# Gates of a hybrid block as 2x2 blocks with seven products in a stage of their own, tokens scaled first, attention and linear attention filled with other projections

## The chip, the core and the metric

The kernel runs on one core of a Trainium2 chip. The metric is the device time of one execution in microseconds (us), the median over runs. The core has five engines that run at the same time, each its own list of instructions in order: TensorE (PE: matmuls and transposes; PEld is its weight load), VectorE (DVE), ScalarE (ACT), GpSimd (POOL) and SyncE (SP, which here only issues DMA transfers). An instruction waits until the tiles it reads are written and the buffer it writes is free.

## The reference, cut to what matters

Sixteen meta tokens and 1024 frames (1040 tokens of width 1024) go through one layer: half a feed-forward block, a mix of attention and gated linear attention, half a feed-forward block.

```python
h = h + 0.5 * swiglu(rmsnorm(h, ffn1_norm), ...)                 # D_FF = 2816
u = rmsnorm(h, mix_norm)                                         # h / rms(h) * gain
(aq, ak, av, gq, gk, gv, gr, g_low, gate_a, gate_b) = split(u @ w_in)
ya = window_sink_attention(aq, ak, av, att_sinks)                # 16 chunks of 64 frames, 8 heads
log_a = log_sigmoid(g_low @ gla_gate_w + gla_gate_b) / 16
og = gated_linear_attention(gq, gk, gv, log_a)                   # 4 heads, running sums of log_a
yb = rmsnorm(og, gla_out_norm) * silu(gr)
mixed = sigmoid(gate_a) * (ya @ w_branch_att) + sigmoid(gate_b) * (yb @ w_branch_gla)
h = h + mixed @ w_out
h = h + 0.5 * swiglu(rmsnorm(h, ffn2_norm), ...)
return rmsnorm(h, final_norm)[:, 16:]
```

`gate_a` and `gate_b` are 1024 columns wide each, the widest parts of `w_in`; `gq` and `gk` have 256, `gv`, `gr` and `aq` 512, `ak` and `av` 128, `g_low` 16.

## The kernel before

Features lie on the 128 partitions, tokens along the rows. A float32 operand is split into a high and a low part, and each product takes three matmuls: high weight by high token, high weight by low token, low weight by high token. In the source this is `mm` (L97, L98, L99; tiles `pj` for a projection, `br` for a branch), with 8 input tiles: a *unit* of one projection tile (128 columns) over 512 tokens is 24 matmuls of 128x512. Tokens come in chunks of 512, 512 and 16 or 512, 256 and 272.

Both feed-forward blocks (FFN1 to about 728 us, FFN2 from about 1350 us) work by 2x2 blocks of weights and tokens with seven products instead of eight (`Seven`, `Group`; L515, tiles `pb`, `pa`, `pd`). The sums of weight blocks come from VectorE or GpSimd, and each sum is split by a ScalarE cast (L291) and a VectorE subtraction (L292).

The mix between them runs so:

1. In the last products of FFN1 (L840) `add_half` (L403) updates `h`, and `Norm.put` (L131) writes gain times `h` as `u2h` and `u2l`. The sums of squares (L862) give the RMS factor only after the first projections (`total`, `spread`), and every projection is multiplied by it on VectorE when it leaves PSUM.
2. K, V, Q of the attention; then 16 attention chunks (`turn`, `scores`, `values`, `attend`), each with one gate-A unit (`fill.pop(0)()`) between its parts. The gate goes to DRAM (`gates`).
3. Attention branch, then `g_low`, `gk`, `gq`, `gv`. `heads[0].decays()` (matmuls `z` L1279, then a chain over ScalarE, VectorE and GpSimd that ends in `kd`, the tile `d` of L1298, in `gq` of L1302 and `gk` of L1304) is issued before the last projections.
4. Linear attention: two pairs of heads, each `begin` (transposes `km`, `kt`), `products(0)`, `state`, and 8 steps. A step has one gate-B unit, then `products(j + 1)` (`at`), then `step(j)` (`go`, `kv`). `heads[1].decays()` is issued after the first `state`.
5. Output gate (`gr`), branch of linear attention, `w_out`, FFN2.

A scheduler orders instructions when the program is built. PSUM has 8 banks, handed out in turn by `bank(...)`. `ttile` takes one of 4 temporary buffers.

Of the kernel before, what the change touches and what calls it, by code (L numbers as in the profile page):

```python
# [35 lines left out]
def hybrid_kernel(  # L36
# [67 lines left out]


    def tiles_of(c0, n):
        return [(t, P if t < S // P else NM) for t in range(c0 // P, (c0 + n + P - 1) // P)]

    class Norm:

        def __init__(self, g, name, pool=None, cols=T):
            self.g, self.name, self.pool, self.cols = g, name, pool, cols
            self.hi = [None] * KT
            self.lo = [None] * KT
            self.acc = None
            self.tot = sml.tile([P, 9], F32, tag="tot", name=f"{name}t", bufs=2)

        def open(self, m):  # L120
            self.hi[m] = atile(f"{self.name}h{m}", F32R, self.pool, self.cols)
            self.lo[m] = atile(f"{self.name}l{m}", F32R, self.pool, self.cols)
            if m == 0:
                self.acc = atile(f"{self.name}q", F32, self.pool, self.cols)

        def put(self, m, c0, n, h):

            g = vec[:, self.g + m:self.g + m + 1]
            hi, lo = self.hi[m][:, c0:c0 + n], self.lo[m][:, c0:c0 + n]
            nc.scalar.activation(hi, h, AF.Copy, scale=g)  # L130
            nc.vector.scalar_tensor_tensor(lo, h, g, hi.bitcast(F32), op0=ALU.mult, op1=ALU.subtract)  # L131

        def total(self, c0, n):

            ps = bank("tot")
            for t, w in tiles_of(c0, n):
                nc.tensor.matmul(ps[0:w, t:t + 1], self.acc[:, t * P:t * P + w], ones[:, 0:1], start=True, stop=True)
            self.root(c0, n, ps)

        def root(self, c0, n, tot):  # L140

            ts = tiles_of(c0, n)
            for lo, hi, w in ((ts[0][0], min(ts[-1][0] + 1, 8), P), (8, ts[-1][0] + 1, NM)):
                if lo < hi:
                    r = self.tot[0:w, lo:hi]
                    nc.scalar.activation(r, tot[0:w, lo:hi], AF.Sqrt, bias=eps_t[0:w, :], scale=1.0 / D)
                    nc.vector.reciprocal(r, r)

        def widen(self, c0, n, dg):

            ts = tiles_of(c0, n)
            for w in (P, NM):
                mine = [t for t, v in ts if v == w]
                if mine:
                    a, k = mine[0] * P - c0, len(mine)
                    nc.vector.tensor_copy(
                        dg[0:w, a:a + k * P].rearrange("p (a b) -> p a b", b=P),
                        self.tot[0:w, mine[0]:mine[0] + k].unsqueeze(2).to_broadcast([w, k, P]))

        def spread(self, c0, n, dg=None):  # L160

            ps = bank("rep")
            if dg is None:
                dg = ttile("dg")
                self.widen(c0, n, dg)
# [1465 lines left out]
```

## Time and profile before

| what | value |
|---|---|
| median of 3 runs | 2053.46 us (2052.05 to 2054.71) |
| the profiled execution | 2056.41 us, of which the span of the trace is 2054.7 us |
| granted TensorE clock, mean over the span | 0.992 |
| busy share of the span | PE 99%, DVE 66%, ACT 41%, POOL 10% |
| instructions | PE 12177, DVE 2305, ACT 1599, POOL 222 |

The span goes from the first to the last instruction; the rest of an execution's time lies around it. A busy share is an average over stages whose limits differ. A granted clock of 1.00 is 2.4 GHz, 0.50 is 1.2 GHz.

### The profile page before, as it was taken

What the parts mean: (1) busy time and instruction counts of PE and PEld (TensorE: products, weight loads), DVE (VectorE), ACT (ScalarE), POOL (GpSimd) and SP (SyncE); (2) the same over time, 40 slices, a digit from 0 to 9 for tenths busy, and PEclk for the clock granted to TensorE, in tenths of its full rate; (3) what the DMA queues carried; (4) which work ended last, traced back from release to release, by engine and by line L of the source; (5) the groups of instructions that cost most, each with busy time, mean ns of one, the idle gap of its engine ahead of it and who ended that gap; (6) DMA issues with size and microseconds to landing.
All of it is one profiled execution on the core that took longest, in us unless ns stands there. A gap on an engine that the chain in (4) does not pass through costs nothing.

```text
span 2054.7 us, 31806 instructions
## 1 busy us (share of the span) xinstructions
PE 2024.0 (99%) x12177; PEld 1801.9 (88%) x12177; DVE 1359.7 (66%) x2305; ACT 835.0 (41%) x1599; POOL 195.2 (10%) x222
## 2 busy tenths in 40 slices
PE   8899999999999999999999999999999999999998
PEld 7899999999999998888897778888888888878888
DVE  5866677666688775774435336568876776757885
ACT  5534444444322354664224323244544544442223
POOL 1000000001223060000100000120000000022212
PEclk9999999999999999999999999999999999999999
DMA  6333344349976231126211225641543443699722
GB/s 206 106 112 128 125 161 161 125 146 343 351 280 221 80 88 54 58 60 187 76 52 57 62 67 175 219 139 44 185 161 123 168 160 125 206 374 347 279 92 83
DMA packets 271690, 317.74 MB, mean 155 GB/s; under 512 B 23975, under 2 KB 187937, under 8 KB 271537
## 3 DMA queue, kind: packets, MB, share of 16 engines
q1 hardware_dynamic: 253888, 254.30, 37.6%
q10 hardware_dynamic: 17296, 61.29, 7.9%
q8 instruction: 96, 1.57, 0.3%
q0 software_dynamic: 352, 0.11, 0.1%
q14 instruction: 58, 0.47, 0.1%
HBM read 208.01 MB, written 107.63 MB: 154 GB/s over the span
## 4 chain that ended last, share of the span: by engine, by line
PE 92%; DMA 4%; DVE 2%; ACT 1%; issue 1%; SPq 0%; DVEq 0%; POOLq 0%; ACTq 0%
PE pb L515 30%; PE pd L515 15%; PE pa L515 7%; PE pj L97 6%; PE pj L98 6%; PE pj L99 6%; PE br L97 1%; PE br L99 1%; PE br L98 1%; PE wo L97 1%; PE wo L98 1%; PE wo L99 1%; PE pd L840 1%; DMA tm<-f2mid 1%; PE tp L1096 1%; DMA f1mid<-kl 1%
## 5 line engine op out<-in xcount | busy, mean ns | idle before, releaser
L515 PE MATMUL pb<-tt,wop 128*128 128x260 f32 (+1 forms) x2016 | 337.8, 321 | 0.0
L515 PEld LDWEIGHTS pb<-tt,wop 128*128 128x128 f32 x2016 | 294.9, 188 | 28.1
L515 PE MATMUL pb<-tm,wop 128*128 128x260 f32 (+1 forms) x1440 | 238.4, 322 | 7.0 <-DVE h L403 3.6
L291 ACT CAST wop<-s 128x512 fp32r<-128x512 f32 x232 | 144.0, 622 | 227.3 <-PE pb L515 97.9
L515 PEld LDWEIGHTS pb<-tm,wop 128*128 128x128 f32 x1440 | 210.4, 191 | 27.1 <-ACT h L458 4.1
L97 PE MATMUL pj<-u2h,whi 128*128 128x512 f32 (+2 forms) x608 | 229.4, 377 | 2.9 <-DVE o L1350 1.7
L98 PE MATMUL pj<-u2l,whi 128*128 128x512 f32 (+2 forms) x608 | 224.5, 369 | 0.0
L99 PE MATMUL pj<-u2h,wlo 128*128 128x512 f32 (+2 forms) x608 | 224.4, 369 | 0.0
L292 DVE TENSOR_TENSOR wop<-s,wop 128x512 fp32r<-128x512 f32 x232 | 166.2, 718 | 87.0 <-ACT wop L291 86.4
L291 ACT CAST wop<-raw 128x512 fp32r<-128x512 f32 x174 | 108.3, 623 | 219.6 <-PE pb L515 104.9
L499 POOL TENSOR_TENSOR s<-raw 128x512 f32<-128x512 f32 x28 | 37.0, 1323 | 1059.9 <-DMA tm<-f1mid 455.2
L97 PEld LDWEIGHTS pj<-u2h,whi 128*128 128x128 f32 x608 | 114.6, 188 | 22.2 <-issue 2.2
L292 DVE TENSOR_TENSOR wop<-raw,wop 128x512 fp32r<-128x512 f32 x174 | 122.2, 704 | 12.8 <-ACT wop L291 12.4
L99 PEld LDWEIGHTS pj<-u2h,wlo 128*128 128x128 f32 x608 | 114.5, 188 | 17.1
L98 PEld LDWEIGHTS pj<-u2l,whi 128*128 128x128 f32 x608 | 114.6, 189 | 15.3
L403 DVE SCALAR_TENSOR_TENSOR h<-pb,h 128x520 f32<-128x520 f32 (+1 forms) x136 | 93.8, 693 | 41.6 <-PE pb L515 39.4
L515 PE MATMUL pd<-tm,wop 128*128 128x260 f32 (+1 forms) x720 | 118.8, 319 | 0.0
L192 ACT CAST whi<-raw 128x1024 fp32r<-128x1024 f32 x58 | 60.8, 1048 | 134.5 <-PE pj L98 76.7
L515 PE MATMUL pb<-tb,wop 128*128 128x260 f32 (+1 forms) x672 | 112.6, 321 | 0.5 <-ACT vec L88 0.5
L515 PEld LDWEIGHTS pd<-tm,wop 128*128 128x128 f32 x720 | 104.4, 189 | 9.5
L515 PE MATMUL pa<-tb,wop 128*128 128x260 f32 (+1 forms) x672 | 112.3, 320 | 0.0
L515 PE MATMUL pd<-tb,wop 128*128 128x260 f32 (+1 forms) x672 | 112.2, 320 | 0.0
(381 smaller groups left out, 3803.6 us busy)
## 6 DMA issues: line engine op xcount, KB each, us to landing
tm<-f1mid ACTq DMA_DIRECT2D x56, 520.0 KB, 6.3
tm<-f2mid ACTq DMA_DIRECT2D x56, 512.0 KB, 5.9
raw<-in_ffn_w_gate SPq DMA_DIRECT2D x42, 512.0 KB, 3.9
raw<-in_ffn_w_up SPq DMA_DIRECT2D x42, 512.0 KB, 3.9
raw<-in_ffn_w_down SPq DMA_DIRECT2D x80, 256.0 KB, 5.2
f1mid<-kh SPq DMA_DIRECT2D x70, 260.0 KB, 2.8
f1mid<-kl SPq DMA_DIRECT2D x70, 260.0 KB, 2.9
f2mid<-kh SPq DMA_DIRECT2D x70, 256.0 KB, 2.9
```

Of the source, the lines that this page charges most:

```text
L97: nc.tensor.matmul(ps, wh[k], xh[k], start=(k == 0), stop=False)
L98: nc.tensor.matmul(ps, wh[k], xl[k], start=False, stop=False)
L99: nc.tensor.matmul(ps, wl[k], xh[k], start=False, stop=(k == n - 1))
L192: nc.scalar.copy(hi[:, 0:cols], raw[:, 0:cols])
L291: nc.scalar.copy(x[:, 0:n], src)
L292: nc.vector.tensor_sub(x[:, n:2 * n], src, x[:, 0:n].bitcast(F32))
L403: nc.vector.scalar_tensor_tensor(hm, ps, 0.5, hm, op0=ALU.mult, op1=ALU.add)
L499: (eng.tensor_add if add else eng.tensor_sub)(a[s], a[x], a[y])
L515: nc.tensor.matmul(ps, y, x[:, c0 + s0:c0 + s0 + sn], start=(first and k == 0 and at == 0), stop=(at == 2 and k == len(cols) - 1), skip_gr ...
L840: nc.tensor.matmul(ps, y, x[:, c0 + s0:c0 + s0 + sn], start=(n == 0), stop=(n == 3 * LAST - 1), skip_group_check=True)
L1096: nc.tensor.transpose(ps[0:k, ga * P:(ga + 1) * P], s.p[:, ga, off:off + k], ident)
```

## The change

- **Tokens scaled first.** The last FFN1 products run half by half (512 + 8 tokens each). The squares are summed on the way, the RMS factor of a half is made (`scales_of_half`, `scales_to_rows`), and `scaled(m, c)` multiplies `h` by gain and factor in place, then splits it (`uh`, `ul`). Evictions of projections no longer multiply.
- **A stage for gates.** GK0, GK1, GV0 run with interleaved tiles (`together`). Sixteen differences of token blocks replace the blocks in place, twelve are split; then GV1, then eight `gate_pair`s make all 16 gate tiles by 2x2 blocks: 7 products of 12 matmuls of 128x512 for each pair, with sums and splits of the weights, two block sums and four sigmoids. Two token tiles are overwritten, and reloaded from DRAM afterwards.
- **Other fills.** Attention's 16 chunks now hold GV2, GV3, GQ, GR and `g_low`; the linear attention holds the attention branch in units of 12 matmuls of 128x512 (5 before, one in each of the first 8 steps, 1 in the first step of the second pair, 2 at the end) and, in four steps of the second pair, the output gate of the first pair (4 transposes each). GK, GQ, GV and GR lie in DRAM in between.

```diff
+    def scaled(m, c):
+        u = ub[m][c]
+        nc.vector.scalar_tensor_tensor(u, u, vec[:, GM + m:GM + m + 1], accs[c], op0=ALU.mult, op1=ALU.mult)
+        for to, at, n in ((c * 512, 0, 512), (S + 8 * c, 512, NM // 2)):
+            hi, lo = u_hi[m][:, to:to + n], u_lo[m][:, to:to + n]
+            nc.scalar.copy(hi, u[:, at:at + n])
+            nc.vector.tensor_sub(lo, u[:, at:at + n], hi.bitcast(F32))
...
+    for c in range(2):
+        for m in range(KT):
...
+                if m == 2:
+                    dgs[0] = scales_of_half(0, double("tot"))
+                if m == 4:
+                    ps = double("rep")
+                    scales_to_rows(0, (ps, ps[:, 512:]), dgs[0])
+                if m > 4:
+                    scaled(m - 5, 0)
...
+    hooks = {k: (lambda k=k: scaled(k, 0)) for k in range(3, KT)}
+    hooks[2] = second_scales
+    together([0, 1], CH_T[0:1], hooks)
+    scales_to_rows(1, (bank("rep"), bank("rep")), dgs[1])
+    for m in range(KT):
+        scaled(m, 1)
+    together([2], CH_T[0:1])
+    together([0, 1, 2], CH_T[1:])
...
+        nc.vector.tensor_sub(b11[k], b12[k], b11[k])
+        nc.vector.tensor_sub(b12[k], b22[k], b12[k])
+        nc.vector.tensor_sub(b22[k], b22[k], b11[k])
+        nc.vector.tensor_sub(b21[k], b21[k], b22[k])
+    for n, bs, first in (("T2", b22, True), ("T1", b11, True), ("T3", b12, False)):
+        for k in range(4):
+            g8.tops[n][k] = g8.halves(g8.operand(first, "tt"), bs[k])
+    hw[3] = ktiles(wt.cut(wt.raw(plain_views[3])))
+    for ch in CH_T:
+        together([3], [ch])
...
+    def gate_pair(m):
...
+        b = product(0)
+        x11, x22 = g8.block("x11"), g8.block("x22")
+        nc.scalar.copy(x11, b)
+        a = product(1)
+        nc.vector.tensor_add(x11, a, x11)
+        g.sums(nc.vector)
+        keep(0, 0, x11, x11)
+        product(2)
...
+    for m in range(0, 16, 2):
...
+        gate_pair(m)
...
-    for m in range(KT):
-        fill += project_units(cols_view(w_in, C_GA + m * P), CH_FR, spill_gate(m, False))
+    for i in (2, 3):
+        us = project_units(cols_view(w_in, C_GV + i * P), CH_T, ev_tok(i))
+        slots += [us[0:1], us[1:3]]
...
+    for p in range(2):
+        for x, src, n in (("k", gk_dram[p], T), ("q", gq_dram[p], S), ("v", gv_dram[2 * p], S), ("w", gv_dram[2 * p + 1], S)):
+            ins[x, p] = atile(f"g{x}{p}")
+            nc.sync.dma_start(out=ins[x, p][:, 0:n], in_=src)
...
-    heads = [Gla(0)]
-    heads[0].decays()
-    heads.append(Gla(1))
-    heads[0].values()
-    heads[1].values()
...
+    heads = [Gla(0), Gla(1)]
+    heads[0].decays()
+    for _ in range(5):
+        fill.pop(0)()
+    for p in range(2):
+        g = heads[p]
+        g.begin()
+        g.products(0)
+        g.state()
+        if p == 0:
+            heads[1].decays()
+        for j in range(8):
+            if j % 2 == 0 or p == 0:
+                if len(fill) > 2:
+                    fill.pop(0)()
+            if p == 1 and j in (1, 3, 5, 7):
+                out_gate(j // 4, CH_FR[(j // 2) % 2:(j // 2) % 2 + 1])
+            if j < 7:
+                g.products(j + 1)
+            g.step(j)
```

Over the whole program TensorE has 96 matmuls of 128x512 fewer (768 of gate units go, 672 of gate pairs come).

On VectorE, the list of the changed kernel before the first matmul of GV1 reads so; `tt` is the split of a difference of token blocks (`h2`), `g` the copy of transposed GV0 tokens, and `wlo_9159` the low weight of GV1.

```order
L229 TENSOR_TENSOR tt_9132<-h2_5957,tt_9132 128x512
L229 TENSOR_TENSOR tt_9135<-h2_5959,tt_9135 128x512
L229 TENSOR_TENSOR tt_9138<-h2_6230,tt_9138 128x512
L229 TENSOR_TENSOR tt_9141<-h2_6232,tt_9141 128x512
L889 COPY g_9069<-vt_9068 128x512
L229 TENSOR_TENSOR tt_9144<-h2_6033,tt_9144 128x512
L229 TENSOR_TENSOR tt_9147<-h2_6035,tt_9147 128x512
L229 TENSOR_TENSOR tt_9150<-h2_6310,tt_9150 128x512
L229 TENSOR_TENSOR tt_9153<-h2_6312,tt_9153 128x512
L126 TENSOR_TENSOR wlo_9159<-raw_9156,whi_9158 128x1024
```

In the kernel before, a projection's low weight had no token work of this kind ahead of it; here all sixteen differences and twelve splits stand ahead of `wlo_9159`.

On TensorE, the linear attention of the kernel before begins so: `km`, `kt` are transposes of `kd` (`d`), and the last `pj` rows of GV stand ahead of them; `z` is the second pair's.

```order
L98 MATMUL pj<-u2l_8653,whi 128x272
L99 MATMUL pj<-u2h_8652,wlo 128x272
L1227 MATMUL vt<-ident,v 128x128 x3
L1311 MATMUL km<-ident,d 16x128
L1317 MATMUL kt<-ident,d 128x128 x8
L1335 MATMUL at<-gq_11346,gk_11345 128x128 x2
L1327 MATMUL kv<-gvm_11244,km 64x128
L1327 MATMUL kv<-gvm_11245,km 64x128
L1279 MATMUL z<-glow,gw 128x384 x2
L1279 MATMUL z<-glow,gw 128x272
```

And in the changed kernel (`br` is a unit of the attention branch; the first pair's `z` stands 60 matmuls `br` ahead of `km`, right behind the last matmul of the attention):

```order
L97 MATMUL br<-qs_10412,whi 128x512
L98 MATMUL br<-qs_10411,wlo 128x512
L1398 MATMUL km<-ident,d 16x128
L1404 MATMUL kt<-ident,d 128x128 x8
L1422 MATMUL at<-gq_12700,gk_12698 128x128 x2
L1414 MATMUL kv<-gvm_12714,km 64x128
L1414 MATMUL kv<-gvm_12715,km 64x128
L1366 MATMUL z<-glow,gw 128x384 x2
L1366 MATMUL z<-glow,gw 128x272
```

What stood between the first pair's `z` and `km` was the projections of GK1, GQ1 and GV; it is now five branch units.

On VectorE, the second pair's decays in the kernel before (the first copy of an output, `o0`, stands behind `d`):

```order
L1285 TENSOR_TENSOR e_12108<-b_12109,e_12108 128x1040
L1286 SCALAR_TENSOR_TENSOR b_12109<-reset_11269,e_12108 128x1040
L915 TENSOR_TENSOR g_12180<-pj_12149,u2q_8387 128x512
L1336 COPY_PREDICATED attb10_11263<-tri_11258,at_12184 128x128
L1336 COPY_PREDICATED attb11_11264<-tri_11258,at_12187 128x128
L1291 COPY dec_12128<-e_12126 128x8
L1295 TENSOR_TENSOR d_12132<-b_12109 128x1024
L1296 TENSOR_SCALAR d_12132<-b_12109 128x16
L1300 TENSOR_TENSOR e_12137<-b_12109 128x1024
L1356 SCALAR_TENSOR_TENSOR st_12205<-st_12103,dec_11511,kv_12202 128x128
L1298 TENSOR_TENSOR d_12132<-gk1_11526,d_12132 128x1040
L1350 COPY o0_12095<-go_12190 128x128
```

and in the changed kernel:

```order
L1372 TENSOR_TENSOR e_12909<-b_12910,e_12909 128x1040
L1313 TENSOR_TENSOR ga_12944<-br_12946,ga_12944 128x512
L1373 SCALAR_TENSOR_TENSOR b_12910<-reset_12733,e_12909 128x1040
L1423 COPY_PREDICATED attb11_12728<-tri_12722,at_12964 128x128
L1382 TENSOR_TENSOR d_12933<-b_12910 128x1024
L1378 COPY dec_12929<-e_12927 128x8
L1383 TENSOR_SCALAR d_12933<-b_12910 128x16
L1387 TENSOR_TENSOR e_12938<-b_12910 128x1024
L1437 COPY o0_12896<-go_12967 128x128
L1385 TENSOR_TENSOR d_12933<-gk1_12706,d_12933 128x1040
L1437 COPY o1_12897<-go_12968 128x128
L1443 SCALAR_TENSOR_TENSOR st_12982<-st_12904,dec_12765,kv_12979 128x128
```

The order is nearly the same; what moved is TensorE's list beside it, where a step's fill is 12 matmuls instead of 24.

## Rows read from the trace of the kernel before

**Rows 1.** The page: busy time of the engines, and the chain that ended last.

```profile
PE 2024.0 (99%) x12177; PEld 1801.9 (88%) x12177; DVE 1359.7 (66%) x2305; ACT 835.0 (41%) x1599; POOL 195.2 (10%) x222
...
PE 92%; DMA 4%; DVE 2%; ACT 1%; issue 1%; SPq 0%; DVEq 0%; POOLq 0%; ACTq 0%
```

**Rows 2.** TensorE's waits: engine, line, releaser, us in total, times, longest.

```profile
PE pb L515 <- DVE h L403: 3.6, 1, 3.6
...
PE pj L97 <- DVE o L1350: 1.7, 1, 1.7
...
PE pj L97 <- DVE h L403: 1.2, 1, 1.2
...
PE tp L1096 <- DVE p L1081: 0.5, 1, 0.5
```

**Rows 3.** Windows: us, busy (x) of five engines, granted clock, DMA, GB/s.

```profile
520.40:527.20 6.80, 6.09 (x28) 6.09 (x29) 4.51 (x7) 3.50 (x7) 2.56 (x2) 0.50 0.98 313
527.20:534.00 6.80, 6.80 (x58) 6.80 (x58) 3.63 (x5) 3.08 (x7) 1.29 (x1) 1.00 0.98 381
...
1104.00:1107.50 3.50, 3.50 (x10) 2.68 (x9) 3.50 (x6) 3.47 (x8) 1.64 (x1) 0.51 0.03 7
...
728.20:731.60 3.40, 2.23 (x13) 2.20 (x13) 3.40 (x7) 2.64 (x6) 0.87 (x3) 1.00 0.42 157
```

**Rows 4.** Window in FFN2, matmuls of seven products (L515): us, busy (x), clock.

```profile
1450.00:1500.00 50.00, 50.00 (x222) 1.00 0.54 179
```

**Rows 5.** Timeline of TensorE: start, us, line, operation, tiles, [idle before].

```profile
729.43 0.41 PE L97 MATMUL pj<-u2h,whi 128*128 128x384 f32 x1 [1.17 <-DVE h L403]
...
1000.73 0.28 PE L99 MATMUL pj<-u2h,wlo 128*128 128x272 f32 x1
...
1001.23 0.40 PE L97 MATMUL pj<-u2h,whi 128*128 128x512 f32 x1
...
1012.15 0.64 PE L1279 MATMUL z<-glow,gw 96*128 96x384 f32 x3
...
1085.85 0.74 PE L1279 MATMUL z<-glow,gw 96*128 96x384 f32 x3
...
1092.32 0.49 PE L1335 MATMUL at<-gq,gk 64*128 64x128 f32 x4
...
1099.84 0.49 PE L1335 MATMUL at<-gq,gk 64*128 64x128 f32 x4
```

**Rows 6.** Timeline of VectorE at four places, same columns.

```profile
97.76 4.96 DVE L292 TENSOR_TENSOR tt<-ub,tt 128x520 fp32r<-128x520 f32 x8
102.64 0.69 DVE L315 TENSOR_TENSOR ub<-ub 128x520 f32<-128x520 f32 x1
...
726.05 0.75 DVE L131 SCALAR_TENSOR_TENSOR u2l<-h,vec,u2h 128x512 fp32r<-128x512 f32 x1
726.71 0.70 DVE L862 TENSOR_TENSOR sums<-sums,sqs 128x520 f32<-128x520 f32 x1
...
1019.31 1.24 DVE L1285 TENSOR_TENSOR e<-b,e 128x1040 f32<-128x1040 f32 x1 [3.41 <-ACT e L1284]
1020.65 2.33 DVE L1286 TENSOR_TENSOR_SCAN b<-reset,e 128x1040 f32<-128x1040 f32 x1
...
1024.19 3.45 DVE L1295 TENSOR_TENSOR d<-b 128x1024 f32<-128x1024 f32 x1
...
1029.31 1.23 DVE L1298 TENSOR_TENSOR d<-gk,d 128x1040 f32<-128x1040 f32 x1
...
1103.36 0.29 DVE L1350 COPY o<-go 128x128 f32<-128x128 f32 x1
```

**Rows 7.** Timeline of ScalarE over the first decays.

```profile
1013.08 1.42 ACT L1280 ACTIVATE e<-z,vec 128x384 f32<-128x384 f32 x3
1014.52 1.28 ACT L1283 ACT_TABLE_LOAD   x1
```

**Rows 8.** Timeline of GpSimd over the first decays.

```profile
1030.94 2.41 POOL L1302 TENSOR_TENSOR gq<-gq,b 128x1024 f32<-128x1024 f32 x1 [4.37 <-ACT b L1301]
```

More of the change, by code (lines that the diff above doesn't have):

```diff
@@ L103, in split @@
         nc.vector.tensor_sub(lo, src, hi.bitcast(F32))
[L106 to L165, printed above, removed]
-            for t, w in tiles_of(c0, n):
-                a = t * P - c0
-                nc.tensor.transpose(ps[:, a:a + w], dg[0:w, a:a + P], ident[0:w, 0:w])
-            nc.scalar.copy(self.acc[:, c0:c0 + n], ps[:, 0:n])
@@ L871, in hybrid_kernel @@
[L871 to L887 removed]
+    CH_T = [(0, 512), (512, 256), (768, 272)]
+    gates = dram.tile([16, P, S], F32, name="gates")
@@ new lines, in ev_tok, with evac, turn @@
+    def ev_tok(i):
+        def evac(ps, c0, n):
+            v = ttile("v")
+            nc.scalar.copy(v[:, 0:n], ps[:, 0:n])
+            fr = min(n, S - c0) // P
+            def turn():
+                pt, g = bank("vt"), ttile("g")
+                for t in range(fr):
+                    nc.tensor.transpose(pt[:, t * P:(t + 1) * P], v[:, t * P:(t + 1) * P], ident)
+                nc.vector.tensor_copy(g[:, 0:fr * P], pt[:, 0:fr * P])
+                nc.sync.dma_start(out=gv_dram[i, :, c0:c0 + fr * P], in_=g[:, 0:fr * P])
+                if c0 + n == T:
+                    nc.tensor.transpose(pt[0:NM, fr * P:fr * P + P], v[:, n - NM:n], ident)
+                    nc.vector.tensor_copy(g[0:NM, fr * P:fr * P + P], pt[0:NM, fr * P:fr * P + P])
+                    nc.sync.dma_start(out=gvm_dram[i], in_=g[0:NM, fr * P:fr * P + P])
+            late.append(turn)
+        return evac
@@ L889, in project_units @@
+    for m in range(0, 16, 2):
+        if m == 14:
+            g8.ring = [w_main] * 6
+        gate_pair(m)
+    for k in range(4):
+        for i, x in enumerate(halves_of(k, 1)):
+            nc.sync.dma_start(out=x.bitcast(F32), in_=b12_dram[k, i])
+    g7.close()
+    r1.close()
+    wt.ws = [w_main]
+    def project_units(views, chunks, evac):
         state = {}
@@ L1138, in hybrid_kernel @@
             values(c // 2 + 1)
-        if fill:
-            fill.pop(0)()
+        for u in slots[c]:
+            u()
         attend(cur)
         cur = nxt
+    run_late()
+    att.close()
     class Frames:
@@ L1403, in ev_r @@
             split(yb[0][i][:, c0:c0 + n], yb[1][i][:, c0:c0 + n], a)
-        project(C_GR + i * P, CH_FR, ev_r)
+    heads = [Gla(0), Gla(1)]
[18 more added lines that the diff above has]
+            g.step(j)
+        g.end()
+    while fill:
+        fill.pop(0)()
+    for c in range(2):
+        for i in (2, 3):
+            out_gate(i, CH_FR[c:c + 1])
+    right.close()
     mx_ = [[atile(f"m{hl}{i}", F32R) for i in range(KT)] for hl in "hl"]
```

428 lines of the change are left out of this document (230 added, 198 removed).

## The prediction

> **What bounds the kernel now.** I read the page first: TensorE is busy for 99% of the span, and 92% of the chain that ended last is its own [rows 1]. So matmul time counts in full, and everything else only where it makes TensorE wait. The waits of TensorE come next: in the part that changes they are few, 1.2 us on the last `h` of FFN1, 0.5 us in attention and 1.7 us on an output copy of the linear attention [rows 2]. Then the granted clock: behind the 3.6 us wait in FFN1 it stands at 0.50 (1.2 GHz) for 6.8 us and is back at 1.00 in the next window; behind the 1.7 us wait it is 0.51 for 3.5 us; behind the 1.17 us wait it stays at 1.00 [rows 2, 3]. A wait of 1.7 us or more thus costs its length and half of 3.4 to 6.8 us: 28 matmuls instead of 58 [rows 3] are about 3.2 us lost. The question for the change is what it takes from TensorE's sum, and where TensorE now waits.
>
> **Gates.** 768 matmuls of 128x512 go, 672 come. In a projection 48 of them run from 1001.23 to 1012.15, 0.2275 us each [rows 5]. In FFN2 222 matmuls of seven products fill 50 us, 0.2252 each [rows 4]. 672 x 0.2252 - 768 x 0.2275 = **-23.4 us**. (By the count alone, 96 x 0.2275, it is -21.8.) A pair is 84 x 0.2252 = 18.9 us on TensorE. Beside it VectorE has 14 sums, splits and block sums at 0.61, from one start to the next (eight in 97.76 to 102.64 [rows 6]), 8.5 us, and ScalarE about 9 us by its casts of like size. Both are covered with half of the pair to spare, so I count nothing there; without the cover it would be up to 1 us for a pair (a rival below). Stores and loads of the pairs (1 MB in, 1 MB out in 18.9 us, 111 GB/s) lie far under the 381 GB/s that a window reached [rows 3].
>
> **Old waits that go.** 1.2 at the end of FFN1, 0.5 in attention, 1.7 plus 0.2 in the linear attention, and half of the 3.5 us behind it, 1.7: **-5.3 us**. In the last FFN1 products the new squares, sums and `scaled` stand on VectorE between the `add_half`s, each shorter than the product beside it.
>
> **From FFN1's end to GV1.** The new vector work meets too little matmul work here. TensorE is done with FFN1 at about 728.9 (728.26 before, where the wait that ends at 729.43 began [rows 5], and 0.6 for the factor's small products put inside). Then 72 matmuls at 0.2275 = 16.4; 144 of 256 and 272 columns, at half a 512 (0.114) and at 0.125 (four in 1000.73 to 1001.23 [rows 5]), 17.2; factor of the second half, transposes of GV0 and pipeline ends, an estimate of 2.1. It would reach GV1 at 764.6. VectorE starts its first `scaled` at about 726.05, where the second-last `put` is now [rows 6]. Ahead of `wlo` of GV1 (as the list in the section on the change shows) stand 16 `scaled` at 0.66 (726.05 to 726.71 [rows 6]) = 10.6, 16 low parts at 0.61 = 9.7, 16 pieces of 8 columns, 1.9 by an estimate of 0.12 each, 16 differences 9.7, 12 splits 7.3, three `add_half` 1.8, and two sums, factor work, one weight split, a copy and the `wlo` itself, 4.3 by their columns. That is 45.3, with 0.9 of VectorE's own waits 46.2: ready at 772.3. The gap is 7.7, of which some 2 us may come out earlier, as waits of the first projections on `scaled`; VectorE sets the end either way. **+7.6 us.** Bounds: +2.5 if VectorE runs 5 us ahead of this, +12.7 if each of 60 operations takes its whole record (0.69 or 0.75 instead of 0.61 or 0.66, 0.085 more). I take the start-to-start value, which eight operations in a row show. Behind a wait of 4 us or more, the clock falls: **+3.2** (0 to 3.4, the one row of such a wait [rows 3]).
>
> **Start of the linear attention.** Before, `kd` had some 70 us of projections as cover between `z` and `km`; it was ready at 1030.54, 18.4 us after `z` started at 1012.15 [rows 5, 6]. Now TensorE has the `z` (0.65) and 60 `br` at 0.2275 (13.65) there. With Z the end of the attention's last matmul, it stands at `km` at Z + 14.3. The chain: the first `abs` at Z + 1.65 (0.93 after `z` before [rows 5, 7], an eviction and casts of the last chunk are ahead of it now); to the subtraction 6.23 before (1013.08 to 1019.31), less a table load of 1.28 [rows 6, 7] that sits ahead of the wait here, 4.95; to the scan 1.34, through it 2.3 [rows 6]; `d` now stands right behind it in the list; from `d` to the product with `k` 5.1 less the 0.4 that a projection's eviction took, 4.7, and 1.23 for it [rows 6]. `kd` is ready at Z + 16.2: a wait of 2.0 at `km`. `at` waits for `gq`, on GpSimd 2.41 long [rows 8] behind another of that length, Z + 18.5, and for `gk` behind it: 1.95. `kv` waits for the copy of `km` behind branch evictions, 1.15. Sum **+5.1** (2 to 8). The reloads of K, Q, V (4 MB) start about 4 us ahead of Z, when the last projection has read `uh`; at 381 GB/s [rows 3] they need 11 us and hide; were they late, they would delay `kd` by what is over.
>
> **The second decays, in steps 0 and 1.** A step's fill is halved: before, one step took 7.52 us (1092.32 to 1099.84 [rows 5]), of which 24 x 0.2275 = 5.46 were fill and 2.06 its own. The chain on VectorE from `z` (1085.85 [rows 5]) to the end of the `o` copy (1103.65 [rows 6]) was 17.8 us; two fills of 5.46 and own work covered all but the 1.7 wait. Here it is 15.8, without two gate evictions, and TensorE has `z` 0.65, 24 `br` 5.46, step 2.06 and about 1 more, 9.2. **+6.7 us** (5 to 8.5). **Clock**: two waits of over 1.7 us lie close together. The first fall is mostly spent in waiting, 1.5; the second costs 3.2. **+4.7** (1.7 to 6.4).
>
> **Small things.** Steps of the second pair without a fill wait on evictions, 0.5 for a vector copy, and the branch starts with loads behind the gate stores: **+3.0** (0.5 to 8), an estimate.
>
> **Sum.** -23.4 - 5.3 + 7.6 + 3.2 + 5.1 + 6.7 + 4.7 + 3.0 = +1.6. The profiled execution took 2056.41 (span 2054.7 and 1.7 around it), 3.0 above the median of the runs; so 2058.0 for a like execution, and **2055 us** for the median. The gain of the products is given back, in waits where vector chains have lost their cover. Of several bounds with their own luck I make 2049 to 2061 its own range.
>
> **Rivals.**
> R1, VectorE is ahead (faster). If five us of the 45 are done before FFN1's end (8 of the 29 operations from the sixteen `scaled` on), or if TensorE meets other small waits first, `wlo` is not late enough to let the clock fall: the two terms, 10.8, become 2.5: 2047. For it: half `scaled` work is interleaved in FFN1's tail, and VectorE is 66% busy only [rows 1]. Against: the list puts all twelve splits ahead of `wlo`.
>
> R2, the clock falls anew in each step (slower). The second pair has one fill, so its eight steps are bursts of 2.06 us between waits of vector copies. If each wait reaches the 1.7 us after which the clock falls [rows 3], 16.5 us of matmuls (8 x 2.06) run at 1.2 GHz and take up to 16.5 more; with some steps out of it 12: 2067. For it: an `o` copy behind long vector operations was what made the 1.7 us wait [rows 2]. Against: the second pair has no decays left beside it, so the copies are short (0.29 [rows 6]), and the 1.17 us wait left the clock alone [rows 3]. The Trainium skill, "TensorE: Matmul & The Clock Gate", section "HAM oscillation — how this bites in real kernels", speaks for this rival: a loop with short bursts of matmuls between waits is throttled again in every round. By that rule the time would be R2's, 2067. The trace of before shows such falls one at a time, never in series.
>
> R3, vector operations cost their whole record where they write what the next one reads (slower): +5.1 at GV1, and some 2 in the linear attention, 2062.
>
> R4, the gates' stage is not at TensorE's pace (the change doesn't do what it says): a stall of 1 us in each of eight pairs, on weight sums or on the banks of `pb`, 8 us: 2063. Against: FFN2 runs 222 matmuls in 50 us with the same groups [rows 4].
>
> **How the numbers follow.** A difference of 0.2% (4.1 us, 2049.4 to 2057.6) is about what a measurement of this kernel can tell from none. Chances: the forecast 0.38 (faster 0.03, same 0.29, slower 0.06); R1 0.32 (faster 0.29, same 0.03); R2 0.15, R3 0.10, R4 0.05, nearly all slower (0.02 the same). Faster 0.32, same 0.34, slower 0.34. The range reaches from R1 with 4 us of luck, 2043, to just under R2, 2066.
>
> **What would show it.** Right: TensorE reaches the first matmul of GV1 with a wait of some 4 us or more on a vector split or its slot, with the clock at 0.50 behind it; the pairs of gates run in 18.9 us without a wait; two to three waits on `d`, `gq` and `attb` or `o` early in the linear attention, 11 to 12 us in sum, and clocks of 0.5 beside them. Wrong: no wait at GV1 (R1); clock below 1.00 through the second pair (R2); starts of vector operations 0.69 apart in the differences (R3); waits on `wop` or `pb` in the pairs (R4). Most fragile is that VectorE's work between 726 and 772 has no gaps beyond 0.9 us and none of its work is done earlier than I place it.

## The result, and the profile after

The changed kernel takes 2061.34 us (median of 5 runs, 2058.29 to 2064.81) against 2054.21 (2052.05 to 2055.49) for the kernel before: ratio 1.0038, 95% interval 1.0022 to 1.0054. It is 7.1 us slower. The forecast was 2055, about the same, with 2049 to 2061 as its own range, 2043 to 2066 as the whole one, and 0.34 on slower. The profiled execution took 2064.81 us, span 2063.1, so 8.4 more than the one of before; 1.5 of that lie ahead of FFN1's end (729.78 against 728.26), a point that moves between 726.9 and 730.6 in the traces of the experiments below.

The page after, the rows that answer to [rows 1]:

```profile
PE 2011.8 (98%) x12084; PEld 1784.1 (86%) x12084; DVE 1397.7 (68%) x2393; ACT 873.6 (42%) x1692; POOL 197.8 (10%) x216
...
PE 87%; DVE 5%; DMA 4%; ACT 2%; issue 1%; POOL 0%; SPq 0%; DVEq 0%; POOLq 0%; ACTq 0%
```

TensorE works 12 us less, and its share of the chain fell from 92% to 87%, VectorE's rose from 2% to 5%. TensorE's waits after (columns as in [rows 2]). The three in [rows 2] that belong to the mix have successors: at FFN1's end 4.6 us, for `o` 4.3, and attention's `tp` for `p` 1.0:

```profile
PE pj L910 <- issue: 4.6, 1, 4.6
...
PE kv L1441 <- DVE o L1437: 4.3, 1, 4.3
PE vt L888 <- ACT v L882: 3.8, 2, 3.2
PE at L1422 <- issue: 2.6, 1, 2.6
...
PE km L1398 <- DVE d L1385: 2.5, 1, 2.5
PE vt L892 <- DVE g L889: 2.5, 2, 1.2
...
PE tp L1207 <- DVE p L1192: 1.0, 3, 0.6
...
PE br L96 <- DVE o L1437: 0.7, 1, 0.7
...
PE pj L912 <- DVE wlo L126: 0.6, 1, 0.6
```

The granted clock beside them, and one window over the eight gate pairs (columns as in [rows 3]):

```profile
733.16:739.99 6.83, 5.63 (x15) 4.50 (x15) 4.89 (x10) 1.98 (x4) 0.00 (x0) 0.50 0.40 118
777.53:784.36 6.83, 6.24 (x16) 4.79 (x15) 1.60 (x3) 0.04 (x1) 0.00 (x0) 0.50 0.34 96
795.24:946.90 151.66, 151.66 (x671) 125.65 (x670) 72.64 (x112) 65.31 (x112) 7.90 (x20) 1.00 0.39 116
1183.72:1193.96 10.24, 6.96 (x23) 5.22 (x22) 8.35 (x13) 5.52 (x9) 1.48 (x1) 0.50 0.57 177
1204.20:1211.03 6.83, 4.89 (x16) 3.13 (x17) 6.83 (x12) 3.75 (x7) 2.36 (x1) 0.50 0.25 76
```

About half of TensorE's busy time in the four windows at 0.50 is lost: 2.8, 3.1, 3.5 and 2.4 us. The pairs are one block of full busy time at 1.00.

From the last matmul of FFN1 to the first of `w_out` it was 574.6 us (728.26 to 1302.9) and is 581.5 (729.78 to 1311.3), 6.8 more. In it the waits of TensorE were 3.5 us and are 24.4, the clock cost 1.7 and costs 11.8. What is left, TensorE's own work at full clock, fell from 569.4 to 545.3, by 24.1. So the saved products are there, and 30.9 us of new waits and lost clock eat them and 7 more.

Where the vector work was late: VectorE at FFN1's end and ahead of GV1, GpSimd at FFN1's end, and ScalarE's cast of GV1's weight.

```profile
727.59 1.20 DVE L807 SCALAR_TENSOR_TENSOR h<-h,vec,sums 128x520 f32<-128x520 f32 x1
728.71 1.87 DVE L811 TENSOR_TENSOR ul<-h,uh 128x512 fp32r<-128x512 f32 x2
730.51 0.69 DVE L340 SCALAR_TENSOR_TENSOR h<-pd,h 128x520 f32<-128x520 f32 x1
731.12 2.42 DVE L811 TENSOR_TENSOR ul<-h,uh 128x512 fp32r<-128x512 f32 x2
733.46 0.69 DVE L340 SCALAR_TENSOR_TENSOR h<-pd,h 128x520 f32<-128x520 f32 x1
...
741.26 0.29 DVE L791 RECIPROCAL r<-r 128x4 f32<-128x4 f32 x2 [3.21 <-ACT r L790]
...
769.74 4.32 DVE L229 TENSOR_TENSOR tt<-h,tt 128x512 fp32r<-128x512 f32 x7
...
776.95 1.25 DVE L126 TENSOR_TENSOR wlo<-raw,whi 128x1024 fp32r<-128x1024 f32 x1
```

```profile
726.36 1.88 POOL L836 TENSOR_TENSOR sums<-sums,sqs 128x520 f32<-128x520 f32 x1 [0.50 <-ACT sums L802]
728.55 1.41 POOL L836 TENSOR_TENSOR sums<-sums,sqs 128x520 f32<-128x520 f32 x1 [0.32 <-ACT sqs L834]
730.57 2.34 POOL L126 TENSOR_TENSOR wlo<-raw,whi 128x1024 fp32r<-128x1024 f32 x1 [0.61 <-ACT whi L125]
```

```profile
771.60 1.05 ACT L125 CAST whi<-raw 128x1024 fp32r<-128x1024 f32 x1 [0.23 <-PE pj L911]
```

The `scaled` and low-part rows at 727.59, 728.71 and 731.12 take 1.20, 1.87 for two and 2.42 for two: each ends 0.55 to 0.65 us, about its own length, after GpSimd's operation beside it is over. The `add_half` at 730.51, which reads PSUM and one tile of SBUF, runs its 0.69 beside GpSimd. The last `add_half` comes at 733.46 and the first projection at 734.36, 4.57 us after FFN1. At 741.26 VectorE has stood 3.21 us for the factor of the second half: its small products `tot` stand on TensorE behind twelve projection matmuls that ran at 1.2 GHz. At 769.74 to 777 come the last splits and then `wlo` of GV1. Most of the wait ahead of GV1 (3.17 of 3.76 us) is for `v`, the tile of the transposes of GV0, which waits for a temporary buffer; `wlo`, ready 1 us after these transposes could start (778.20 and 777.23), would have held TensorE as long.

The same in the decays of the linear attention:

```profile
1176.84 1.23 DVE L1382 TENSOR_TENSOR d<-b 128x1024 f32<-128x1024 f32 x1
...
1178.05 2.38 DVE L1383 TENSOR_SCALAR d<-b 128x16 f32<-128x16 f32 x1
...
1186.21 2.47 DVE L1313 TENSOR_TENSOR ga<-br,ga 128x512 f32<-128x512 f32 x4
1188.60 0.27 DVE L1400 COPY km<-km 16x128 f32<-16x128 f32 x1
...
1203.88 0.22 DVE L1383 TENSOR_SCALAR d<-b 128x16 f32<-128x16 f32 x1
...
1205.15 0.28 DVE L1437 COPY o<-go 128x128 f32<-128x128 f32 x1
```

```profile
1177.98 2.42 POOL L1380 TENSOR_TENSOR qi<-gq,e 128x1024 f32<-128x1024 f32 x1 [8.80 <-ACT e L1376]
```

At 1178.05 an operation on 16 columns takes 2.38 us beside GpSimd's product of 2.42; in the second decays the same one takes 0.22. At 1186.21 the four evictions of branch units stand behind the whole chain, then `km`'s copy; at 1205.15 an `o` copy stands behind the second chain.

### The profile page after: what moved, and what is told of

Same layout as the page of the kernel before. It is cut to its first block, busy times and chain, and to the rows that moved or that the text cites. A ratio compares the mean times of both kernels' runs of the same rounds, so it can differ in the third digit from the quotient of the medians.

```text
span 2063.1 us, 31910 instructions
## 1 busy us (share of the span) xinstructions
PE 2011.8 (98%) x12084; PEld 1784.1 (86%) x12084; DVE 1397.7 (68%) x2393; ACT 873.6 (42%) x1692; POOL 197.8 (10%) x216
## 3 DMA queue, kind: packets, MB, share of 16 engines
q8 instruction: 95, 1.56, 0.3%
## 4 chain that ended last, share of the span: by engine, by line
PE 87%; DVE 5%; DMA 4%; ACT 2%; issue 1%; POOL 0%; SPq 0%; DVEq 0%; POOLq 0%; ACTq 0%
PE pb L453 34%; PE pd L453 17%; PE pa L453 8%; PE pj L96 2%; PE pj L97 2%; PE pj L98 2%; PE wo L96 1%; PE wo L98 1%; PE wo L97 1%; PE br L96 1%; PE br L98 1%; PE br L97 1%; PE pd L827 1%; PE pg L628 1%; PE pg L630 1%
## 5 line engine op out<-in xcount | busy, mean ns | idle before, releaser
L453 PE MATMUL pb<-tt,wop 128*128 128x260 f32 (+1 forms) x2208 | 385.2, 327 | 0.0
L453 PEld LDWEIGHTS pb<-tt,wop 128*128 128x128 f32 x2208 | 330.9, 188 | 35.5
L229 DVE TENSOR_TENSOR wop<-s,wop 128x512 fp32r<-128x512 f32 x264 | 186.5, 713 | 113.3 <-ACT wop L228 112.7
L453 PE MATMUL pd<-tt,wop 128*128 128x260 f32 (+1 forms) x768 | 136.4, 329 | 0.0
L453 PEld LDWEIGHTS pd<-tt,wop 128*128 128x128 f32 x768 | 115.9, 188 | 13.1
L453 PEld LDWEIGHTS pb<-tb,wop 128*128 128x128 f32 x672 | 97.9, 188 | 9.9 <-ACT vec L87 0.6
L453 PEld LDWEIGHTS pd<-tb,wop 128*128 128x128 f32 x672 | 97.9, 188 | 9.3
L453 PEld LDWEIGHTS pa<-tb,wop 128*128 128x128 f32 x672 | 97.8, 188 | 9.3
L436 DVE TENSOR_TENSOR s<-raw 128x512 f32<-128x512 f32 x94 | 64.6, 688 | 54.7 <-DMA raw<-in_ffn_w_up 52.6
L96 PE MATMUL pj<-uh,whi 128*128 128x512 f32 (+2 forms) x256 | 94.9, 371 | 0.0
```

Of the source, the lines that this page charges most:

```text
L96: nc.tensor.matmul(ps, wh[k], xh[k], start=(k == 0), stop=False)
L229: nc.vector.tensor_sub(x[:, n:2 * n], src, x[:, 0:n].bitcast(F32))
L436: (eng.tensor_add if add else eng.tensor_sub)(a[s], a[x], a[y])
L453: nc.tensor.matmul(ps, y, z[:, s0:s0 + sn], start=(first and k == 0 and at == 0), stop=(at == 2 and k == len(cols) - 1), skip_group_check= ...
```

## The experiments

Each edit is made on the changed kernel. Times are medians; the ratio is to the kernel before, run beside it. "Stage" is a stretch of the profiled execution: FFN1's last matmul to the first gate matmul (64.4 us in the changed kernel), last gate matmul to `z` (219.3), `z` to the last output-gate transpose (100.7). Kernels with no edit in the first show 62.7 to 64.5 there, so it is good to a microsecond or two; those with none in the last show 100.6 to 101.0.

| run | us | ratio (95%) | stage |
|---|---|---|---|
| changed kernel | 2061.3 | 1.0038 (1.0022 to 1.0054) | 64.4 / 219.3 / 100.7 |
| e1_own_slot | 2055.1 | 1.0003 (0.9994 to 1.0012) | 55.8 / 219.1 / 100.6 |
| e2_slot_v | 2054.8 | 1.0002 (0.9994 to 1.0011) | 55.9 / 219.2 / 100.8 |
| e3_scaled_later | 2060.4 | 1.0027 (1.0017 to 1.0036) | 61.9 / 219.2 / 101.0 |
| e4_no_pool | 2057.4 | 1.0017 (1.0007 to 1.0026) | 59.1 / 219.2 / 100.6 |
| e5_more_fill | 2062.4 | 1.0035 (1.0023 to 1.0047) | 63.1 / 219.3 / 97.7 |
| e6_two_covers | 2057.8 | 1.0023 (1.0006 to 1.0039) | 64.5 / 219.3 / 101.4 |
| e7_idle | 2064.0 | 1.0045 (1.0033 to 1.0057) | 62.7 / 219.3 / 105.9 |
| e8_best | 2044.2 | 0.9947 (0.9934 to 0.9960) | 54.1 / 216.5 / 94.4 |
| e9_o_act | 2060.8 | 1.0034 (1.0022 to 1.0046) | 63.0 / 219.3 / 101.8 |
| e10_vec_br | 2060.7 | 1.0039 (1.0024 to 1.0053) | 62.7 / 219.3 / 98.8 |
| e11_best2 | 2042.0 | 0.9943 (0.9932 to 0.9955) | 54.1 / 216.5 / 96.1 |
| e12_all | 2045.4 | 0.9949 (0.9935 to 0.9963) | 52.6 / 216.4 / 109.3 |

**GV1's weight in its own buffer (e1).** The index sends it to a pool with free buffers; before, it took the two that GK0's weight holds. The cut is also issued earlier in the source, ahead of the differences and splits instead of behind them.

```diff
+    wt.i = 4
+    hw[3] = ktiles(wt.cut(wt.raw(plain_views[3])))
     together([2], CH_T[0:1])
...
-    hw[3] = ktiles(wt.cut(wt.raw(plain_views[3])))
```

Expected: 

> GV1's weight gets a buffer of its own and is cut before the differences; nothing else. In the changed kernel TensorE stood 3.17 us for the transposes of GV0 (their tile v waits on ScalarE for a temporary buffer whose store is late) and 0.59 us for the low weight, and the clock was at 0.50 for 6.83 us behind it. Theory A (two things end within 1 us of each other, the temporary buffer and the weight): only the 0.6 us goes, the 3.2 us and the clock stay, 2060 to 2061. Rival B (the prediction's account: VectorE's list ahead of the low weight sets it): the wait at GV1 falls below 1 us, no clock fall, 2054 to 2056.

Measured 2055.1, 6 us less; rival B holds. VectorE and a window of this run:

```profile
742.76 1.21 DVE L126 TENSOR_TENSOR wlo<-raw,whi 128x1024 fp32r<-128x1024 f32 x1
...
770.62 3.10 DVE L229 TENSOR_TENSOR tt<-h,tt 128x512 fp32r<-128x512 f32 x5
```

```profile
763.00:782.50 19.50, 19.27 (x138) 17.94 (x137) 16.61 (x29) 11.72 (x24) 0.15 (x1) 1.00 0.20 69
```

`wlo` of GV1 now stands at 742.76, ahead of all splits; those run beside GV1's matmuls, at full clock. The wait on `v`, which I took for a cause of its own, went with it, because the scheduler then puts those transposes later. In the changed kernel ScalarE's half of the cut began only at 771.60, when the last matmul with GK0's weight had freed the buffer, and the source issues the cut behind the twelve splits. The edit takes away both, and no run has one without the other. The buffer alone does not explain the lateness: by an estimate from these rows `wlo` could have followed at 772.65 (771.60 and 1.05) and been done at 773.9, 4.3 us before the 778.20 that it took behind the splits.

**Token tiles of GV with buffers of their own (e2).** As e1, and `v` from a pool of two instead of the four temporaries.

```diff
-            v = ttile("v")
+            v = vp.tile([P, TW], F32, tag="v", name="v")[:, 0:512] if i < 2 else ttile("v")
```

Expected: 

> As the run before, and GV0's and GV1's token tiles get a pool of two buffers of their own. Theory A: both causes are gone, so 3.8 us of waits and 3 us of clock go: 2054 to 2056, with the vector splits now hidden behind GV1's 72 matmuls. Rival B: nothing beyond the run before. Rival C: the wait reappears in the first pair of gates, on the splits of the third product; then within 2 us of the changed kernel.

Nothing beyond e1 (2054.8, stage 55.9): rival B. Once the weight is early the temporaries hold up nothing; whether they do without it (the 3.17 us for `v` in the changed kernel) this run, made on top of e1, does not test.

**Second and third token tile scaled later (e3).**

```diff
-                if m > 4:
-                    scaled(m - 5, 0)
+                if m == 7:
+                    scaled(0, 0)
...
-    hooks = {k: (lambda k=k: scaled(k, 0)) for k in range(3, KT)}
-    hooks[2] = second_scales
+    hooks = {k: (lambda k=k: scaled(k, 0)) for k in range(1, KT)}
+    hooks[2] = lambda: (second_scales(), scaled(2, 0))
```

Expected: 

> In FFN1's tail only the first token tile is scaled; the second and third come between the first projections. The changed kernel's first projection waits 4.57 us, because the last add_half stands behind them, and the clock is at 0.50 for 6.83 us; the factor of the second half (tot) then runs late and VectorE stands idle for 3.21 us. Theory A (the early wait feeds the vector chain through tot): first wait about 2 us, no clock fall or one of half the length, the idle 3.2 us shrinks to under 1, 2056 to 2058. Rival B (VectorE's sum of work ends at GV1 whatever happens before): the wait moves from the first projection to GV1, 2060 to 2063.

The first wait fell from 4.57 to 1.56 (and 0.86, 0.66 behind it), and the clock did not fall there. But the stage is only 1 to 2.5 us shorter: the waits at GV1 (2.53, 0.52, 1.51) and the fall behind them stayed. The median moved 1 us, within the spread. So the first wait is paid once more at GV1 for the larger part, as rival B has it (2060 to 2063).

**No GpSimd at FFN1's end (e4).**

```diff
-                (nc.vector if c == 0 or m >= KT - 2 else nc.gpsimd).tensor_add(accs[c], accs[c], sq)
+                nc.vector.tensor_add(accs[c], accs[c], sq)
...
-    hw[2] = ktiles(wt.cut(raws[2], eng=nc.gpsimd))
+    hw[2] = ktiles(wt.cut(raws[2]))
```

Expected: 

> No GpSimd work in FFN1's tail: its four sums of squares and the low weight of GV0 go to VectorE. In the changed kernel three vector operations beside GpSimd's took 1.20, 1.79 and 2.34 us where their like take 0.7. Theory A (a vector operation with two inputs in SBUF stands until GpSimd's is done): these 3.2 us go, against 3.6 us of new vector work, some of it where VectorE was idle; add_half of the last tile comes 1 to 2 us earlier, first wait 2.5 to 3.5, 2057 to 2061. Rival B (vector operations are only slow there by chance or by waits): VectorE is 3.6 us longer, 2063 to 2066.

VectorE in this run (two of the rows that answer to those above):

```profile
727.17 0.75 DVE L807 SCALAR_TENSOR_TENSOR h<-h,vec,sums 128x520 f32<-128x520 f32 x1
...
729.67 0.76 DVE L811 TENSOR_TENSOR ul<-h,uh 128x512 fp32r<-128x512 f32 x2
```

The same operations take 0.75 and, for two, 0.76. With six operations more on VectorE (five sums, one more than expected, and the low weight) the stage is 5.3 us shorter, and the first wait is 2.28 instead of 4.57, a little under what theory A gave; the clock stays at 1.00 behind it, and VectorE does not stand for the factor. Theory A holds.

**More fill ahead of `km` (e5).**

```diff
-    for _ in range(5):
+    for _ in range(8):
         fill.pop(0)()
```

Expected: 

> Eight branch units instead of five stand between the first pair's z and km; the steps have three fewer. In the changed kernel TensorE waits there 2.48 (km), 2.64 (at) and 0.64 us (kv), and the clock is at 0.50 for 10.24 us, of which some 7 are matmuls, 3.5 lost. Theory A (the chain of the decays lacks cover): these 9 us go and steps without a fill lose nothing, as those of the second pair show: 2051 to 2054. Rival B (work only moves: the steps that lose their fill now wait on vector copies): 2057 to 2060.

The wait at `km` is gone, and others came. TensorE's waits in this run:

```profile
PE at L1422 <- DVE ga L1313: 2.9, 1, 2.9
...
PE kv L1414 <- DVE km L1400: 2.5, 1, 2.5
```

`at` waits for the evictions of branch units, `kv` for the copy of `km` behind them: all on VectorE behind the chain, and a unit has to load its gate into one of four temporaries first. The stage is 3 us shorter, the median (2062.4) no lower than the changed kernel's and above both theories. Cover alone was not what was short: TensorE stands until VectorE's list gets to what frees its banks.

**Two covers (e6).** Seven units, `begin`, the second pair's decays, five units, then the first products.

```diff
-    for _ in range(5):
+    for _ in range(7):
         fill.pop(0)()
...
         g.begin()
+        if p == 0:
+            heads[1].decays()
+            for _ in range(5):
+                fill.pop(0)()
         g.products(0)
         g.state()
-        if p == 0:
-            heads[1].decays()
```

Expected: 

> Seven branch units ahead of the first pair's begin; then the second pair's decays, and five units ahead of its first products; two units in steps, two at the end. Theory A (both chains of decays lack cover; 4.32 and 0.66 us of waits in steps 0 and 1, and 2.4 us of a second fall of the clock go too): 16 us less than the changed kernel, 2044 to 2048. Rival B (the second fall and new waits come back in the bare steps of the first pair, bursts of 2.06 us, clock at 0.50 in them): 2055 to 2065.

2057.8, 3.5 less than the changed kernel, with a wide spread (2053.2 to 2073.0). The waits of the linear attention fell from 11.4 to 7.0 us, and in the profiled execution the clock took it back. TensorE's last wait ahead of the steps without a fill, and a window in them:

```profile
1222.33 0.58 PE L1422 MATMUL at<-gq,gk 64*128 64x128 f32 x2 [0.99 <-DVE o L1437]
```

```profile
1222.60:1239.70 17.10, 17.10 (x78) 11.79 (x78) 6.82 (x28) 5.43 (x27) 0.00 (x0) 0.50 0.09 30
```

TensorE waits for nothing in the window, and runs it at 1.2 GHz. The longest wait of this stage, 3.30 us up to 1211.21, had cost 3.4 us at 0.50, and the clock was back at 1.00 for 6.8 us; the long fall came behind a wait of 0.99. Rival B. The intervals of this run and of the changed kernel overlap, so the 3.5 us are not shown as a gain.

**Idle matmuls in the waits (e7).** Twelve matmuls of 96x512 whose product is thrown away ahead of `km`, twelve ahead of the first `at`.

```diff
+    def idle(n):
+        ps = bank("idle")
+        for k in range(n):
+            nc.tensor.matmul(ps, gw[:, 0:P], glow[0:3 * GR, 0:512], start=(k == 0), stop=(k == n - 1))
...
+        if p == 0:
+            idle(12)
         g.begin()
+        if p == 0:
+            idle(12)
         g.products(0)
```

Expected: 

> Twelve matmuls more (96x512, the product thrown away) ahead of km, and twelve ahead of the first at, in the place of the two waits of 2.48 and 2.64 us; they bring nothing to the output. Theory A (the clock's fall has a price of its own beside the wait): no clock at 0.50 at the start of the linear attention, 3 us less than the changed kernel, 2057.5 to 2059.5, with fills that last 0.3 us longer than the waits. Rival B (the fall lies in time that the next wait would take anyway): the waits grow by what the clock gives back, 2060 to 2062.

2064.0, above both theories. A failed experiment: the extra bank that they take makes `kt` wait for a branch eviction in the place of `at`, and the clock is at 0.50 for 13.7 us instead of 10.24. The wait:

```profile
PE kt L1404 <- DVE ga L1313: 3.1, 1, 3.1
```

It doesn't tell what the fall costs by itself. It does show again that the bank is what TensorE waits for.

**Output copies on ScalarE (e9).**

```diff
-                nc.vector.tensor_copy(self.o[i][:, c:c + P], po)
+                nc.scalar.copy(self.o[i][:, c:c + P], po)
```

Expected: 

> The copies of the linear attention's outputs (o, 32 of 128x128) go from VectorE to ScalarE. In the changed kernel TensorE waits 4.32 and 0.66 us for one that stands behind the second pair's decays in VectorE's list, and the clock is at 0.50 for 6.83 us beside it. Theory A (what releases TensorE is late because it queues behind the chain in one list): these 5 us and some 2.4 of the clock go, 2054 to 2057. Rival B (the copies of attb and the state st in the same list take its place): at most 2 us less, 2059 to 2062.

The 4.32 us wait is gone (0.6 left), but `st` and `attb` from the same list take 1.6 and 1.5, and the clock falls for 10.2 us instead of 6.8:

```profile
PE go L1432 <- DVE st L1443: 1.6, 1, 1.6
PE go L1429 <- DVE attb L1423: 1.5, 1, 1.5
```

2060.8: rival B.

**Decays' products on VectorE, the first five branch units (those without a gate loaded) out by ScalarE (e10).**

```diff
-            nc.gpsimd.tensor_mul(self.qi[:, 0:S], q[:, 0:S], e[:, 0:S])
+            nc.vector.tensor_mul(self.qi[:, 0:S], q[:, 0:S], e[:, 0:S])
...
+        if g is None:
+            g = ttile("ga")
+            nc.scalar.copy(g[:, 0:n], ps[:, 0:n])
+            nc.sync.dma_start(out=ya_dram[m, :, c0:c0 + n], in_=g[:, 0:n])
+            return
```

Expected: 

> The two products of each pair's decays that GpSimd makes (qi, gq) go to VectorE, and the first five branch units leave PSUM by a ScalarE copy (their product with the gate is made later, ahead of the last branch). More fill ahead of km had brought new waits for the branch's evictions (at for ga 2.94, km's copy behind ga 2.49 us). Theory A (TensorE waits for banks and copies that queue on VectorE, and VectorE stands beside GpSimd: 2.38 us for an operation of 0.22): km's wait 2.48 becomes 1.3 to 1.8, at's 2.64 and kv's 0.64 together under 1, the clock's fall is shorter; 4 to 6 us less, 2055 to 2058. Rival B (VectorE's own work decides, now four products of 1.2 us longer, and five in the last branch): waits of the same length at other places, 2060 to 2063.

```profile
PE br L96 <- DVE o L1447: 3.2, 1, 3.2
PE kv L1451 <- DVE o L1447: 2.5, 1, 2.5
...
PE km L1408 <- DVE d L1395: 1.9, 1, 1.9
...
PE at L1432 <- DVE gk L1401: 1.7, 1, 1.7
```

`km` 2.48 to 1.9, `at` 2.64 to 1.7, `kv`'s 0.64 gone, but `o`'s copies now stand behind two products more (2.5 and 3.2). The stage is 1.9 us shorter; 2060.7, rival B, no difference to be measured.

**Together (e8, e11, e12).** e8 has e1, e4, e6 and the meta-token transposes of GV ahead of the frames' copy (they waited 1.2 us twice for it, `vt` L892 above):

```diff
+                if c0 + n == T:
+                    nc.tensor.transpose(pt[0:NM, fr * P:fr * P + P], v[:, n - NM:n], ident)
                 nc.vector.tensor_copy(g[:, 0:fr * P], pt[:, 0:fr * P])
                 nc.sync.dma_start(out=gv_dram[i, :, c0:c0 + fr * P], in_=g[:, 0:fr * P])
                 if c0 + n == T:
-                    nc.tensor.transpose(pt[0:NM, fr * P:fr * P + P], v[:, n - NM:n], ident)
```

Expected: 

> Five edits together: GV1's weight in a buffer of its own and cut early, no GpSimd work in FFN1's tail, meta-token transposes of GV ahead of the copy of the frames (two waits of 1.2 us and small ones in attention), and the two covers of the run before. Theory A (each cause stands alone, so what they give adds up: 6 to 8 at GV1, 2.5 in attention, 16 in the linear attention): 2034 to 2040. Rival B (they share one bound, VectorE, so that half comes back): 2044 to 2050.

2044.2, ten below the kernel before: the three stages are 10.3, 2.8 (the transposes) and 6.3 us shorter than the changed kernel's. That is the fast end of rival B: what the edits give does not add up in full. e11 has the first three of these with e9 and e10, and fills as in the changed kernel.

Expected: 

> The three edits ahead of the linear attention that the eighth run had (own buffer for GV1's weight, no GpSimd in the tail, meta tokens first) with the edits of the two runs above, and the fills where the changed kernel has them. Theory A: 12 to 14 us less than the changed kernel by the first three, and 9 to 13 by the others: 2035 to 2041. Rival B: only the first three count, 2048 to 2051.

2042.0, the best version here, 11.8 under the kernel before; 1 us above theory A and well under rival B. The waits that are left in the mix, of this run:

```profile
PE pj L911 <- ACT uh L810: 2.3, 1, 2.3
...
PE km L1410 <- DVE d L1397: 1.9, 1, 1.9
...
PE at L1434 <- DVE gk L1403: 1.7, 1, 1.7
PE go L1441 <- DVE attb L1435: 1.5, 1, 1.5
```

So e9 and e10, which alone changed the last stage by +1.1 and -1.9 us and the time by nothing, go with 4.6 us of it together, in one profiled execution each (of these some 1.7 are clock, 13.7 us at 0.50 instead of 17.1). The waits show why: each had removed one of the things that queue in one list, and the next took its place. No run has e11 without these two, so their share of its 2042.0 is not measured. e12 is e11 with the diff of e6, 6 and 6 in the place of 7 and 5.

Expected: 

> The run before with the fills moved as in the sixth: six branch units ahead of the first pair's begin, six between the second pair's z and the first products, two in steps, two at the end. In the run before 5.9 us of waits were left in the linear attention (km 1.94, at 1.70 and 0.47, go 1.53) and 13.6 us at 0.50. Theory A (with the evictions off VectorE's list, cover now counts): these waits fall under 2 us and the clock's fall to one of 3.4 us, 2035 to 2039. Rival B (the bare steps of 2.06 us make the clock fall, as in the sixth run, for 17 us): 2043 to 2050.

2045.4, slower than e11 (2042.0), with two of seven runs 11 us longer (2055.3, 2055.8). The profiled one is of these:

```profile
1202.09 0.49 PE L1441 MATMUL go<-gv,attb 128*128 128x128 f32 x2 [2.85 <-DVE attb L1435]
```

```profile
1202.50:1253.70 51.20, 51.20 (x238) 35.10 (x237) 18.93 (x51) 18.99 (x95) 0.00 (x0) 0.50 0.16 50
```

And e8:

```profile
1205.00:1240.00 35.00, 33.44 (x263) 23.57 (x261) 23.84 (x82) 16.32 (x68) 0.00 (x0) 1.00 0.24 83
```

A wait of 2.85 us at 1199.24 was the last; from 1202.5 on TensorE waits for nothing, and for 51.2 us of bare steps (steps without a fill) the clock stays at 0.50. In e8, behind a wait of 3.52 us and 3.4 us at 0.50, the same bare steps ran at 1.00 in its profile. The last stage is 13.2 us longer than e11's (109.3 against 96.1), with 4.6 us of waits in it instead of 5.9. The other five runs (2043.6 to 2046.5) left no trace; their mean granted clock, 0.989 to 0.990, is a little under the 0.991 to 0.993 of e11's runs. By its time, rival B; its mechanism is seen in one execution, of the two long ones.

## Why the prediction was right in its range and short in its sum

The mechanism was as put: the products' gain is real and given back in waits on vector chains. The sum was +1.6 us and the mix measured +6.8; the median, 2061.3, lies in the whole range but just above the forecast's own, 2049 to 2061. Term by term, in the profiled execution:

| term | predicted | measured |
|---|---|---|
| gates, 96 matmuls fewer | -23.4 | -22.0 (152.7 for 672; all of TensorE's work -24.1) |
| old waits and clock | -5.3 | -5.3 |
| FFN1's end to GV1, waits | +7.6 | +9.0 |
| its clock | +3.2 | +5.9 |
| start of the linear attention | +5.1 | +5.8 |
| second decays | +6.7 | +5.0 |
| clock of both | +4.7 | +5.9 |
| small things | +3.0 | +4.7 (attention 3.5, others 1.2) |

Five terms measured 0.7 to 2.7 us more than predicted, 7.7 in sum; TensorE's own work and the second decays came out 0.7 and 1.7 better. The largest miss is the clock between FFN1's end and GV1.

**The step that failed** is the sum for VectorE ahead of GV1: "with 0.9 of VectorE's own waits 46.2: ready at 772.3". It was ready at 778.2, 5.9 later. It stood 3.2 us beside GpSimd (1.20, 1.87 and 2.42 for what takes 0.75, 0.76 and 0.76 in e4), of which I had none, and 3.2 for the factor of the second half, where I had 0.9 for all waits. The start-to-start prices held: the differences stand 0.60 apart. R3 (whole records) is out; its 2062 was near the measured time by luck, by another cause. e4 shows the first part, taken away. That the term for the wait, +7.6 for 9.0, is off by less than the 5.9 is because TensorE was late to GV1 too, by its own first wait and its clock.

**The first wait** I had at 2 us, without a price of its own, since VectorE sets the end either way. e3 bears that out for most of it, but the wait was 4.57, the clock fell there too, and the slowed matmuls sat ahead of `tot`, on which VectorE waited. The loss went round through both engines. So two falls of the clock, not one: 5.9 instead of 3.2.

**R1** came out wrong as put (VectorE was behind, not ahead). **R4**: the pairs ran at 100% busy, right. **The linear attention** was right to under 1 us in each wait of its start (`km` at Z + 16.6, foreseen 16.2, `at` Z + 20.6, foreseen 18.9; the three waits 2.48, 2.64 and 0.64, foreseen 2.0, 1.95 and 1.15). There the stand beside GpSimd was inside the row that the chain was taken from (3.45 in [rows 6] for what takes 1.23 in the changed kernel); no row that was used for FFN1's end had it. But the reason I gave, lost cover, is only a part: in e5 and e7 the evictions that free TensorE's banks, in e9 `st` and `attb`, stand in VectorE's list behind the chains. For `at` in the changed kernel itself the profile names no releaser. **R2**: the changed kernel's bare steps, of the second pair, ran at 1.00, so it did not come. In e6 and e12 it did, for 17.1 and 51.2 us in one execution each, behind one wait each (0.99 and 2.85 us) and not anew in each step as R2 had it. The Trainium skill, "TensorE: Matmul & The Clock Gate", section "HAM oscillation — how this bites in real kernels", has the throttling come back with each wait of a loop. The trace of e12 differs: one wait, then 51.2 us at 0.50 with no wait at all.

**Where the 7 us lie**: e1 alone takes 6 of them back, with one weight cut early into a buffer of its own. That the low weight of GV1 stands behind twelve splits was seen; that it need not stand there was not.

## What to carry to other kernels

A saving on the busiest engine is worth what the handovers around it leave: list what releases its banks and weights, and in whose queue that stands, before counting cover. Removing one of several late releases from the same list can gain nothing in the time until the others go too (e9 and e10 alone +1.1 and -1.9 us of their stage, together -4.6). A weight's cut belongs ahead of vector work that can run beside the matmuls, and it needs a buffer that is free by then: e1 does both and gains 6 us.
